# Start addresses of weight and activation tiles, and the place of each mixer unit's second transposition, in a two-block transformer kernel

## The chip, the cores and the metric

The kernel runs on one core of a Trainium2 chip, as one program. The metric is device time in microseconds (us): the median of a few executions. One further execution was taken with the hardware profiler, and all rows below come from it. Engines are named as the profile names them: PE is TensorE (PEld its weight loads), DVE is VectorE, ACT is ScalarE, POOL is GpSimd, SP is SyncE, whose queue starts most transfers.

## The reference, cut to what matters

256 tokens of width 2048 go through two transformer blocks, all in float32.

```
def first_block(x, mem, ...):
    xn = _rmsnorm(h, norm_mix)
    y = xn @ w_in                                  # 2048 x 7472
    mixed = concat(_gdn_group(y[..., :GDN_COLS]),  # gated delta rule, 8 heads of 128
                   _rwkv_group(y[..., GDN_COLS:])) # RWKV-7, 16 heads of 64
    h = h + mixed @ w_out
    h = h + _cross_attention(_rmsnorm(h), _rmsnorm(mem), wq, wk, wv, wo)
    h = h + square(relu(_rmsnorm(h) @ mlp_w_up)) @ mlp_w_down     # 2048 x 8192 x 2048
    return _rmsnorm(h, norm_final)

def second_block(x, ...):
    qa, ka, va, ga, qb, kb, vb, gb = split(x @ w_in)              # 2048 x 8192
    y = concat(dilated(qa, ka, va) * silu(ga), neighbourhood(qb, kb, vb) * silu(gb))
    return _layer_norm(ALPHA * x + y @ w_out)
```

## The kernel before, in words

Almost all of the work is the product of 256 tokens with about 390 MB of weights, which are read once. A weight piece of 256 rows by 512 columns comes in by one transfer (`raw`, three buffers). `piece` splits it in two float32r tiles: ACT writes the rounded half `whi`, DVE the rest `wlo = raw - whi`. Activations stand split in the same way (`ah`/`al`, `uh`/`ul`), and each product is three matmuls: high by high, high by low, low by high. A matmul has a stationary operand (128 columns that LDWEIGHTS puts into the array) and a moving one, which streams past it.

There are two forms. In `ws_parts` ("weights stationary") a 128x128 block of `whi` or `wlo` is stationary and 256 tokens of `ah` or `al` move: 256 columns a matmul, output by channel. In `as_parts` ("activations stationary") 128 tokens of `ah`, `al`, `uh` or `ul` are stationary and 512 columns of `whi` or `wlo` move. In the profile the moving operand is named first: `acc<-ah,whi` is the first form, `acc<-whi,ah` the second.

The pool `fix` lives through the whole program and holds `raw`, `whi`, `wlo`, one set of activation tiles and small constants. Other pools (`xn`, `work`, `act2`, `mlp`, `blk2`, `y`) are opened and closed by stage, and each begins where the pools that are open leave off.

From about 120 to 620 us the input projection runs interleaved with six mixer units: `rwkv_quarter(0)`, `(1)`, `gdn_half(0)`, `rwkv_quarter(2)`, `(3)`, `gdn_half(1)`. A unit is a chain of small steps on all engines. It is a generator whose yields (`yield cost, lat`) tell a planner in the same function how much PE work it has just issued and how much other PE work is to be put in before its next step; the planner fills with parts of the projection (0.66 each, six matmuls). PE's order is the one that this planner writes out. The other engines' orders are chosen by a scheduler when the program is built. Each unit ends with two halves of 128 tokens (c = 0 and 1). After the last product of a half (`op` in a quarter, `og` in a half) the output is normalized: DVE takes sums, POOL takes a power (`var` or `sso`, in `powc`), DVE multiplies, and then `finish(c)` transposes the result on PE (tiles `onp` or `ot`). `inverse_blocks` is a run of 62 operations on POOL (`Xt`, `X`), and the one of the following unit stands in the same POOL queue.

Of the kernel before, what the change touches and what calls it, by code (L numbers as in the profile page):

```python
# [9 lines left out]
F32 = mybir.dt.float32  # L10
F32R = mybir.dt.float32r
# [52 lines left out]
def block_kernel(tc, a, out, dbg=None, stop=99):  # L64
# [4 lines left out]
    def pool(name, space=None):  # L69
        kw = {"space": space} if space is not None else {"reuse_waits": "tile"}  # L70
        return ctx.enter_context(tc.tile_pool(name=name, bufs=1, **kw))

    def open_pool(name, side=None):
        cm = tc.tile_pool(name=name, bufs=1, side=side, reuse_waits="tile")
        return cm.__enter__(), lambda: cm.__exit__(None, None, None)

    fix = pool("fix")
    PS = {}

# [41 lines left out]

    last = {}

    def piece(W, r0, nk, cols):

        n = sum(c[1] for c in cols)
        with tc.high_priority():
            raw = fix.tile([128, nk, n], F32, name="raw", tag="raw", bufs=3)
            for c0, m, d in cols:
                nc.sync.dma_start(out=raw[:, :, d:d + m],  # L130
                                  in_=W[r0:r0 + nk * 128, c0:c0 + m].rearrange("(k p) n -> p k n", p=128))
            hi = fix.tile([128, nk, n], F32R, name="whi", tag="whi", bufs=3)
            lo = fix.tile([128, nk, n], F32R, name="wlo", tag="wlo", bufs=3)
            last["act"] = act(hi, raw)
            last["dve"] = nc.vector.tensor_tensor(out=lo, in0=raw, in1=hi.bitcast(F32), op=SUB)  # L135
        return hi, lo
# [8 lines left out]
    cst = fix.tile([128, K_END], F32, name="cst")  # L145
    nc.scalar.dma_start(out=cst[:, 0:128], in_=a["cst"][:, 0:128])
    pr0 = fix.tile([16, 128], F32, name="pr0")
    xnp, close_xn = open_pool("xn")
    xt = [xnp.tile([128, 2, 512], F32, name=f"xn{q}") for q in range(4)]
    lora_cols = [(7184, 288, 0), (4096, 16, 288)]  # L150
    first = []
    pr3 = fix.tile([75, 128], F32, name="pr3")
    nc.gpsimd.memset(pr3, 0.0)
    with tc.manual_schedule(engines={nc.sync.engine}):
        xq = pieces(a["x"], xt, (0,))
        nc.sync.dma_start(out=pr0, in_=a["norm_mix"][0].rearrange("(r c) -> r c", c=128))
        for qs in ((1,), (2,), (3,)):
            xq = pieces(a["x"], xt, qs)
            first.append(piece(a["w_in"][0], 256 * len(first), 2, lora_cols))
        nc.sync.dma_start(out=cst[:, 128:], in_=a["cst"][:, 128:])  # L160
        nc.sync.dma_start(out=pr3[0:26, :], in_=a["rwkv_mu"][0, 0:3328].rearrange("(r c) -> r c", c=128))
        nc.sync.dma_start(out=pr3[26:27, 0:32], in_=a["rwkv_mu"][0:1, 3328:3360])
        for i, n in enumerate(("rwkv_k_k", "rwkv_k_a", "rwkv_r_k", "rwkv_ln_w", "rwkv_ln_b", "rwkv_a0")):
            src = a[n][0].rearrange("h c -> (h c)") if n == "rwkv_r_k" else a[n][0]
            nc.sync.dma_start(out=pr3[27 + 8 * i:35 + 8 * i, :], in_=src.rearrange("(r c) -> r c", c=128))
# [48 lines left out]
    def act_tiles(where=None, bufs=8):  # L214

        hs, ls = [], []
        for _ in range(bufs // 2):
            h = (where or fix).tile([128, 4, T], F32R, name="ah", tag="act", bufs=bufs)
            l = (where or fix).tile([128, 4, T], F32R, name="al", tag="act", bufs=bufs)
            hs += [h[:, i, :] for i in range(4)]  # L220
            ls += [l[:, i, :] for i in range(4)]
        return hs, ls
# [17 lines left out]
                tr(p[:, t * 128:(t + 1) * 128], src(t, k // 4)[:, (k % 4) * 128:(k % 4) * 128 + 128])  # L240
            split(p, hs[k], ls[k], gain[:, k:k + 1])

    def by_channel(p, name):

        n = p.shape[0]
        q = pst([128, 128], "parp")
        tr(q[:, 0:n], p)
        o = fix.tile([128, n], F32, name=name)
        nc.vector.tensor_copy(o, q[:, 0:n])
        return o  # L250

    gains = {"mix": by_channel(pr0, "par0")}

    def ws_parts(W, cols, xh, xl, emit, kts=None, r0=0, needs=(), first=()):


        total = sum(c[1] for c in cols)
        n = -(-total // 128)
        acc = [mmt([128, 2, T], "acc") for _ in range((n + 1) // 2)]
        kts = kts or list(range(len(xh)))  # L260
        nk = 2
        for i in range(0, len(kts), nk):
            hi, lo = first[i // nk] if i // nk < len(first) else piece(W, r0 + kts[i] * 128, nk, cols)
            for c in range(n):
                cc = slice(c * 128, min(c * 128 + 128, total))
                o = acc[c // 2][0:cc.stop - cc.start, c % 2, :]
                for j in range(nk):
                    k = kts[i + j]
                    mm(o, hi[:, j, cc], xh[k], start=(i + j == 0 and c % 2 == 0), stop=False)
                    mm(o, hi[:, j, cc], xl[k], start=False, stop=False)  # L270
                    mm(o, lo[:, j, cc], xh[k], start=False, stop=(i + j == len(kts) - 1 and (c % 2 == 1 or c == n - 1)))
                yield PART
        yield from needs
        with tc.high_priority():
            for c in range(n):
                emit(c, acc[c // 2][:, c % 2, :])
# [39 lines left out]
    w_in = a["w_in"][0]  # L316
# [3 lines left out]
    r0 = rstd(xq, "r0")  # L320
# [34 lines left out]
    normw = bcast("normw", a["gdn_norm_w"][0], 128)  # L355


    work_p, close_work = open_pool("work")

    def wk(shape, name, bufs=1, dt=F32):  # L360
# [193 lines left out]
    def rwkv_quarter(qt):  # L554
# [149 lines left out]
        for c in range(2):  # L704
            rp_ = pst([128, 4, 64], "rp_")
            for h in range(4):
                if c == 1 and h % 2 == 0:
                    mm(rp_[:, h:h + 2, :], AR[:, h // 2, 1, 0, :], zs[:, h // 2, :], stop=False)
                mm(rp_[:, h, :], L[h][:, 1, :], vtok[:, c, h, :], start=(c == 0), stop=(c == 0 or h % 2 == 1))
            rs = wk([128, 4, 64], "rs")  # L710
            act(rs, rp_)
            yield 0.45 + 0.4 * c, 1.3
            up = pst([128, 4, 64], "up")
            for h in range(4):
                mm(up[:, h, :], tinv[:, c * 4 + h, :], rs[:, h, :])
            us = wk([128, 4, 64], "us")
            nc.vector.tensor_copy(us, up)
            yield 0.45, 1.5
            op = pst([128, 4, 64], "op")
            for h in range(4):  # L720
                if c == 1 and h % 2 == 0:
                    mm(op[:, h:h + 2, :], AR[:, h // 2, 1, 1, :], zs[:, h // 2, :], stop=False)
                mm(op[:, h, :], L[h][:, 0, :], us[:, h, :], start=(c == 0), stop=False)
                mm(op[:, h, :], L[h][:, 2, :], vtok[:, c, h, :], start=False, stop=(c == 0 or h % 2 == 1))
            if c == 0:
                zp = pst([128, 2, 64], "zp")
                for h in range(4):
                    i, e = h // 2, slice(64 * (h % 2), 64 * (h % 2) + 64)
                    mm(zp[e, i, :], btok[:, h, :], us[:, h, :], stop=False)
                    mm(zp[e, i, :], ktok[:, h, :], vtok[:, 0, h, :], start=False)  # L730
                for h1 in range(2):
                    e = slice(64 * h1, 64 * h1 + 64)
                    tt(zs[e, :, e], zp[e], zsc[e].unsqueeze(2).to_broadcast([64, 2, 64]), MUL)

            mean = wk([128, 4], "mean", bufs=2)
            nc.vector.tensor_reduce(out=mean, in_=op, axis=AX.X, op=ADD)
            ts(mean, mean, 1.0 / 64, MUL)
            o_ = wk([128, 4, 64], "oc")
            oc.append(o_)
            tt(o_, op, mean.unsqueeze(2).to_broadcast([128, 4, 64]), SUB)  # L740
            osq = wk([128, 4, 64], "rs")
            act(osq, o_, AF.Square)
            var = wk([128, 4], "var", bufs=2)
            nc.vector.tensor_reduce(out=var, in_=osq, axis=AX.X, op=ADD)
            ts(var, var, 1.0 / 64, MUL, 64e-5, ADD)
            powc(var, var, mhalf[:, 0:4])
            tt(o_, o_, var.unsqueeze(2).to_broadcast([128, 4, 64]), MUL)
            if c == 0:
                yield 1.5, 0.5
                for i in range(2):  # L750
                    lmats(1, i)
                    yield 1.3, 2.5 * i
                finish(0)
                yield 0.22, 0
            else:
                yield 0.9, 7.0
                finish(1)
                yield 0.22, 0
        done.add(("end", f"q{qt}"))
# [33 lines left out]
    def gdn_half(hf):  # L793
# [156 lines left out]
        tt(o_[1], p, o_[1], ADD)  # L950
        norm(1)
        done.add(("gq", hf))
        yield 2.2, 9.0
        finish(1)
        done.add(("gz", hf))
        yield 0.45, 0
# [461 lines left out]
            attention(grp, hf)  # L1418
    close_at()
    yp, close_y = open_pool("y")  # L1420
    for more, x in zip(act_tiles(yp, 4), (yh, yl)):
        x += more
    for grp in range(2):
# [75 lines left out]
```

## Time and profile before

| | |
|---|---|
| time, median of 3 runs | 2284.04 us (2282.37 to 2285.6) |
| the profiled execution's own time | 2280.03 us |
| its span, first to last instruction | 2278.3 us |
| PE busy | 2215.0 us, 97% of the span |
| DVE, ACT, POOL busy | 1385.3, 1119.9, 272.5 us |
| mean granted PE clock | 0.990 of full speed |

Busy time counts an instruction from its start to its (modelled) end; matmuls overlap each other, so their durations add up to more than PE's busy time. What a matmul takes of the span is the distance from its start to the next one's.

### The profile page before, as it was taken

To read this page: it belongs to the slowest core of one execution; us is meant where nothing else is said; L and a number is where in the kernel's file an instruction comes from. 1 tells how busy PE (TensorE), PEld (TensorE's weight loads), DVE (VectorE), ACT (ScalarE), POOL (GpSimd) and SP (SyncE) were. 2 spreads that over 40 slices of the span, in tenths; PEclk is the share of its full clock that TensorE was granted. 3 is DMA by queue.
4 is the path that set the end of the run, shared out by engine and by line. 5 is a ranking of instruction groups with operands and counts; after the bars stand their busy time and mean duration, and the time that the engine had idled before them with its cause. 6 is when DMAs were issued, how large, how long until landed. Compare 5 with 4: busy or idle time off the path is not lost.

```text
span 2278.3 us, 39054 instructions
## 1 busy us (share of the span) xinstructions
PE 2215.0 (97%) x15506; PEld 2013.3 (88%) x15506; DVE 1385.3 (61%) x2236; ACT 1119.9 (49%) x1802; POOL 272.5 (12%) x540
## 2 busy tenths in 40 slices
PE   8999999899999999999999999999999999999996
PEld 8998888889988899889998898898888999889975
DVE  5576676675644556555554455455456677777765
ACT  5455454554444545454444444344344565656542
POOL 0027255345200000000000000000000000022101
PEclk9999999999999999999999999999999999999998
DMA  6554244344466554456665665565556666665553
GB/s 209 185 162 123 94 153 130 105 147 129 143 211 205 183 171 148 155 181 183 189 188 185 186 188 189 186 186 188 189 183 197 197 189 188 183 181 167 178 191 130
DMA packets 229060, 391.77 MB, mean 172 GB/s; under 512 B 39886, under 2 KB 47820, under 8 KB 228493
## 3 DMA queue, kind: packets, MB, share of 16 engines
q1 hardware_dynamic: 227297, 385.63, 55.0%
q10 hardware_dynamic: 1036, 3.58, 0.4%
q8 instruction: 121, 1.98, 0.4%
q14 instruction: 62, 0.51, 0.1%
q0 software_dynamic: 544, 0.07, 0.0%
HBM read 386.25 MB, written 2.97 MB: 171 GB/s over the span
## 4 chain that ended last, share of the span: by engine, by line
PE 85%; POOL 5%; DVE 3%; DMA 2%; ACT 2%; issue 2%; SPq 0%; POOLq 0%; ACTq 0%; DVEq 0%
PE acc L96 78%; POOL X L102 2%; POOL Xt L102 2%; DVE wlo L135 1%; DMA raw<-in_w_in_dram 1%; DMA nb<-scr 1%; PE s2p L96 1%; PE o2p L96 1%; PE t2p L178 1%; PE xo L96 1%; PE xs L96 0%; PE tp L178 0%; ACT whi L99 0%; DMA kT<-in_mem_dram 0%; DVE h L111 0%
## 5 line engine op out<-in xcount | busy, mean ns | idle before, releaser
L135 DVE TENSOR_TENSOR wlo<-raw,whi 128x1024 fp32r<-128x1024 f32 (+1 forms) x696 | 852.2, 1225 | 718.0 <-ACT whi L99 711.8
L99 ACT ACTIVATE whi<-raw 128x1024 fp32r<-128x1024 f32 (+1 forms) x696 | 734.2, 1056 | 884.4 <-PE acc L96 771.6
L96 PE MATMUL acc<-ah,whi 128*128 128x256 f32 x3120 | 883.7, 284 | 2.2 <-DVE ey L102 1.2
L96 PE MATMUL acc<-ah,wlo 128*128 128x256 f32 x3120 | 872.0, 280 | 3.4 <-DVE wlo L135 3.3
L96 PE MATMUL acc<-al,whi 128*128 128x256 f32 x3120 | 874.8, 281 | 0.0
L96 PEld LDWEIGHTS acc<-ah,whi 128*128 128x128 f32 x3120 | 588.0, 188 | 7.6 <-issue 2.3
L96 PEld LDWEIGHTS acc<-ah,wlo 128*128 128x128 f32 x3120 | 586.3, 188 | 4.9 <-DVE wlo L135 4.8
L96 PEld LDWEIGHTS acc<-al,whi 128*128 128x128 f32 x3120 | 587.8, 188 | 1.4 <-issue 0.9
L96 PE MATMUL acc<-wlo,ah 128*128 128x512 f32 x704 | 278.7, 396 | 0.0
L96 PE MATMUL acc<-whi,al 128*128 128x512 f32 x704 | 278.4, 396 | 0.0
L96 PE MATMUL acc<-whi,ah 128*128 128x512 f32 x704 | 268.7, 402 | 4.0 <-DVE qky L102 2.6
L96 PE MATMUL acc<-wlo,uh 128*128 128x512 f32 x512 | 202.4, 395 | 0.0
L96 PE MATMUL acc<-whi,ul 128*128 128x512 f32 x512 | 202.3, 395 | 0.0
L96 PE MATMUL acc<-whi,uh 128*128 128x512 f32 x512 | 182.5, 395 | 0.0
L96 PEld LDWEIGHTS acc<-whi,ah 128*128 128x128 f32 x704 | 132.3, 189 | 34.5 <-DVE qky L102 2.8
L96 PEld LDWEIGHTS acc<-whi,al 128*128 128x128 f32 x704 | 132.6, 188 | 31.7
L96 PEld LDWEIGHTS acc<-wlo,ah 128*128 128x128 f32 x704 | 133.0, 189 | 30.3
L96 PEld LDWEIGHTS acc<-wlo,uh 128*128 128x128 f32 x512 | 96.0, 188 | 23.4
L96 PEld LDWEIGHTS acc<-whi,ul 128*128 128x128 f32 x512 | 96.1, 188 | 23.2
L96 PEld LDWEIGHTS acc<-whi,uh 128*128 128x128 f32 x512 | 95.9, 187 | 23.3
L102 POOL TENSOR_TENSOR Xt<-X,nb 128x60 f32<-128x60 f32 (+24 forms) x186 | 76.4, 411 | 181.8 <-DMA nb<-scr 163.5
L1342 POOL MEMSET klz<- 64x256 f32 x8 | 2.5, 307 | 714.9 <-DMA raw<-in_w_in_dram 714.6
(523 smaller groups left out, 1858.5 us busy)
## 6 DMA issues: line engine op xcount, KB each, us to landing
raw<-in_w_in_dram SPq DMA_DIRECT2D x240, 512.0 KB, 3.8
raw<-in_mlp_w_up_dram SPq DMA_DIRECT2D x128, 512.0 KB, 3.7
raw<-in_mlp_w_down_dram SPq DMA_DIRECT2D x128, 512.0 KB, 3.8
raw<-in_w_out_dram SPq DMA_DIRECT2D x64, 512.0 KB, 4.4
raw<-in_xattn_wk_dram SPq DMA_DIRECT2D x32, 512.0 KB, 3.8
raw<-in_xattn_wv_dram SPq DMA_DIRECT2D x32, 512.0 KB, 4.9
raw<-in_xattn_wq_dram SPq DMA_DIRECT2D x32, 512.0 KB, 4.1
raw<-in_xattn_wo_dram SPq DMA_DIRECT2D x32, 512.0 KB, 3.7
```

The lines of the kernel that those rows point to most:

```text
L96: nc.tensor.matmul(o, l, r, start=start, stop=stop)
L99: return nc.scalar.activation(o, i, f, **kw)
L102: (eng or nc.vector).tensor_tensor(out=o, in0=x, in1=y, op=op)
L135: last["dve"] = nc.vector.tensor_tensor(out=lo, in0=raw, in1=hi.bitcast(F32), op=SUB)
L178: nc.tensor.transpose(o, i, ident[0:n, 0:n])
L1342: nc.gpsimd.memset(kl[other, e, :].bitcast(F32), 0.0)
```

## The change

Three things are changed. (1) `whi` and `wlo` are allocated 256 B longer per partition, and `piece` has an offset `o` in elements: where weights are stationary (`ws_parts`, and the first pieces) the view begins 56 elements, that is 224 B, into the tile; in `as_parts` it begins at 0. (2) Fillers (`shift`) of 160, 96 and 128 B, and a small tile that is allocated earlier, put `fix`'s big tiles and the pools behind it at multiples of 256 B. (3) Two yields before `finish(1)` ask for more work ahead: 7.0 becomes 9.0 in a quarter, 9.0 becomes 13.0 in a half.

```diff
+    def shift(where, nbytes):
+        if nbytes:
+            where.tile([128, nbytes // 4], F32, name=f"shift{nbytes}")
...
-    def piece(W, r0, nk, cols):
+    def piece(W, r0, nk, cols, o=0):
...
-            hi = fix.tile([128, nk, n], F32R, name="whi", tag="whi", bufs=3)
-            lo = fix.tile([128, nk, n], F32R, name="wlo", tag="wlo", bufs=3)
+            hi, lo = (fix.tile([128, nk * n + 64], F32R, name=x, tag=x, bufs=3)[:, o:o + nk * n]
+                      .rearrange("p (k n) -> p k n", k=nk) for x in ("whi", "wlo"))
...
     pr0 = fix.tile([16, 128], F32, name="pr0")
+    par0 = fix.tile([128, 16], F32, name="par0")
+    shift(fix, 160)
...
-            first.append(piece(a["w_in"][0], 256 * len(first), 2, lora_cols))
+            first.append(piece(a["w_in"][0], 256 * len(first), 2, lora_cols, 56))
...
-            hi, lo = first[i // nk] if i // nk < len(first) else piece(W, r0 + kts[i] * 128, nk, cols)
+            hi, lo = first[i // nk] if i // nk < len(first) else piece(W, r0 + kts[i] * 128, nk, cols, 56)
...
+    shift(fix, 96)
     work_p, close_work = open_pool("work")
...
             else:
-                yield 0.9, 7.0
+                yield 0.9, 9.0
                 finish(1)
...
-        yield 2.2, 9.0
+        yield 2.2, 13.0
         finish(1)
...
     yp, close_y = open_pool("y")
+    shift(yp, 128)
```

Where the two built programs put the operands, as the remainder of the start address by 256 B (all steps inside a tile are multiples of 512 B, so the remainder is the same for every matmul of a line; "distance" is stationary less moving, by 256):

| matmuls | moving, stationary, distance before | after |
|---|---|---|
| weights stationary, 256 columns (all stages) | 96, 32, 192 | 0, 224, 224 |
| activations stationary, tiles in `act2`, `mlp` (`w_out`, `wo`, `w_down`) | 32, 0, 224 | 0, 0, 0 |
| activations stationary, tiles in `fix` (z, `wv`, v of block 2) | 32, 96, 64 | 0, 0, 0 |
| activations stationary, tiles in `blk2`, `y` (last projection) | 32, 0 or 128, 224 or 96 | 0, 0, 0 |
| cross-attention scores `xs` | 96, 64, 224 | 0, 64, 64 |
| block 2 scores `s2p` | 128, 128, 0 | 128, 128, 0 |

On PE the instructions are the same, and the mixer units' are moved. At the end of the first quarter (`op` is its last product, `onp` the second transposition, `gamp` belongs to the following unit), before, with 66 matmuls of the projection left out or shown between `op` and `onp`:

```order
L96 MATMUL op<-us,og 128x64
L96 MATMUL op<-p2d,og 128x64
L96 MATMUL acc<-ah,whi 128x256
...
L96 MATMUL acc<-ah,wlo 128x256
L178 MATMUL onp<-cst,oc 128x128 x2
L96 MATMUL gamp<-cst,g 128x128 x4
```

and after, with 84 between them:

```order
L101 MATMUL op<-us,og 128x64
L101 MATMUL op<-p2d,og 128x64
L101 MATMUL acc<-ah,whi 128x256
...
L101 MATMUL acc<-ah,wlo 128x256
L186 MATMUL onp<-cst,oc 128x128 x2
L101 MATMUL gamp<-cst,g 128x128 x4
```

So 18 projection matmuls have moved ahead of the transposition, and with it of all that stands behind. It is 18 in the second and third quarter too, 6 in the fourth (66 become 72), and 36 in both halves (84 become 120, between `og` and `ot`).

On POOL the scheduler has put one power in another place. In the third quarter, the power of the second half (`var`) stands before behind seven pairs of the following unit's inverse (`Xt`, `X`):

```order
L680 AFFINE_SELECT og<-og 128x2x128
L102 TENSOR_TENSOR Xt<-X,nb 128x31
L102 TENSOR_TENSOR X<-X,Xt 128x31
...
L102 TENSOR_TENSOR Xt<-X,nb 128x2x25
L102 TENSOR_TENSOR X<-X,Xt 128x2x25
L182 TENSOR_TENSOR var<-var,cst 128x4
L102 TENSOR_TENSOR Xt<-X,nb 128x2x24
```

and after it stands ahead of all of them:

```order
L687 AFFINE_SELECT p2c<-p2c 128x128
L689 AFFINE_SELECT p2c<-p2c 128x2x128
L687 AFFINE_SELECT og<-og 128x128
L689 AFFINE_SELECT og<-og 128x2x128
L190 TENSOR_TENSOR var<-var,cst 128x4
L107 TENSOR_TENSOR Xt<-X,nb 128x31
L107 TENSOR_TENSOR X<-X,Xt 128x31
```

In the fourth quarter the same power moves the other way: before, the last two pairs of the inverse stand behind it,

```order
L102 TENSOR_TENSOR X<-X,Xt 128x8x3
L182 TENSOR_TENSOR var<-var,cst 128x4
L102 TENSOR_TENSOR Xt<-X,nb 128x8x2
L102 TENSOR_TENSOR X<-X,Xt 128x8x2
L102 TENSOR_TENSOR Xt<-X,nb 128x8
L102 TENSOR_TENSOR X<-X,Xt 128x8
```

and after, they stand ahead of it:

```order
L107 TENSOR_TENSOR X<-X,Xt 128x8x3
L107 TENSOR_TENSOR Xt<-X,nb 128x8x2
L107 TENSOR_TENSOR X<-X,Xt 128x8x2
L107 TENSOR_TENSOR Xt<-X,nb 128x8
L107 TENSOR_TENSOR X<-X,Xt 128x8
L190 TENSOR_TENSOR var<-var,cst 128x4
```

## Rows read from the trace of the kernel before

**Rows 1.** The page: PE's busy time, and the chain's shares by engine

```profile
PE 2215.0 (97%) x15506; PEld 2013.3 (88%) x15506; DVE 1385.3 (61%) x2236; ACT 1119.9 (49%) x1802; POOL 272.5 (12%) x540
...
PE 85%; POOL 5%; DVE 3%; DMA 2%; ACT 2%; issue 2%; SPq 0%; POOLq 0%; ACTq 0%; DVEq 0%
```

**Rows 2.** Groups by shape, whole span: count | busy us, mean ns | idle before

```profile
L96 PE MATMUL acc<-ah,whi 128*128 128x256 f32 x3104 | 879.3, 284 | 2.2 <-DVE ey L102 1.2 <-ACT whi L99 0.9
L96 PE MATMUL acc<-al,whi 128*128 128x256 f32 x3104 | 870.5, 281 | 0.0
L96 PE MATMUL acc<-ah,wlo 128*128 128x256 f32 x3104 | 868.3, 280 | 3.4 <-DVE wlo L135 3.3
...
L96 PE MATMUL acc<-whi,al 128*128 128x512 f32 x704 | 278.4, 396 | 0.0
...
L96 PE MATMUL acc<-whi,ul 128*128 128x512 f32 x512 | 202.3, 395 | 0.0
...
L96 PE MATMUL s2p<-k,q 128*128 128x256 f32 x64 | 16.9, 284 | 0.0
...
L96 PE MATMUL xs<-kv,qx 128*128 128x256 f32 x96 | 14.2, 280 | 0.0
```

**Rows 3.** The chain in order of time, three stretches: start us, us, what

```profile
587.34 5.65 PE acc L96 x48
...
595.22 9.53 PE acc L96 x84
...
841.67 2.24 PE xs L96 x19
...
979.71 22.40 PE acc L96 x96
```

**Rows 4.** Groups by shape in 650 to 740 us, and at two form changes

```profile
L96 PE MATMUL acc<-whi,al 128*128 128x512 f32 x128 | 50.6, 395 | 0.0
...
L96 PE MATMUL acc<-whi,al 128*128 128x512 f32 x1 | 0.4, 389 | 0.0
...
L96 PE MATMUL acc<-whi,al 128*128 128x512 f32 x1 | 0.4, 398 | 0.0
```

**Rows 5.** PE's timeline at four second transpositions: start us, us [idle before <-releaser]

```profile
245.45 0.33 PE L178 MATMUL onp<-cst,oc 128*128 128x128 f32 x1 [2.85 <-DVE oc L102]
...
389.08 0.59 PE L178 MATMUL ot<-cst,og 128*128 128x128 f32 x2 [3.43 <-DVE og L111]
...
448.30 0.66 PE L178 MATMUL onp<-cst,oc 128*128 128x128 f32 x2 [4.86 <-DVE oc L102]
...
545.36 0.41 PE L178 MATMUL onp<-cst,oc 128*128 128x128 f32 x2 [2.01 <-DVE oc L102]
```

**Rows 6.** Timeline of POOL and DVE ahead of the last two

```profile
439.32 0.60 POOL L102 TENSOR_TENSOR Xt<-X,nb 128x31 f32<-128x31 f32 x1 [10.93 <-DMA nb<-scr]
...
442.43 0.20 DVE L108 TENSOR_SCALAR var<-var 128x4 f32<-128x4 f32 x1
...
446.61 1.02 POOL L182 TENSOR_TENSOR var<-var,cst 128x4 f32<-128x4 f32 x1
...
447.66 0.49 DVE L102 TENSOR_TENSOR oc<-oc,var 128x256 f32<-128x256 f32 x1 [2.58 <-POOL var L182]
...
543.73 1.02 POOL L182 TENSOR_TENSOR var<-var,cst 128x4 f32<-128x4 f32 x1
...
546.53 0.22 POOL L102 TENSOR_TENSOR X<-X,Xt 128x8 f32<-128x8 f32 x1
```

**Rows 7.** Stretches: us, busy by engine (count), granted PE clock, DMA share, GB/s

```profile
391.00:394.00 3.00, 3.00 (x16) 3.00 (x15) 3.00 (x8) 1.04 (x3) 0.00 (x0) 0.50 0.37 109
448.40:452.30 3.90, 3.90 (x19) 3.90 (x20) 1.03 (x3) 2.15 (x4) 3.19 (x10) 0.50 0.00 0
```

**Rows 8.** The fourth quarter's `xd`: durations min/median/max ns, first to last start

```profile
L96 PE MATMUL py<-xd,nt x32: 191/191/212, 499.1 to 499.6; 32*32 32x32 f32 x32
...
L99 ACT ACTIVATE xd<-Xt x4: 307/320/323, 483.9 to 486.0; 32x64 f32<-32x64 f32 x4
```

More of the change, by code (lines that the diff above doesn't have):

```diff
@@ L241, in transposed, with by_channel @@
             split(p, hs[k], ls[k], gain[:, k:k + 1])
-    def by_channel(p, name):
+    def by_channel(p, name, o=None):
         n = p.shape[0]
@@ L247, in by_channel @@
         tr(q[:, 0:n], p)
-        o = fix.tile([128, n], F32, name=name)
+        o = o if o is not None else fix.tile([128, n], F32, name=name)
         nc.vector.tensor_copy(o, q[:, 0:n])
         return o
-    gains = {"mix": by_channel(pr0, "par0")}
+    gains = {"mix": by_channel(pr0, "par0", par0)}
     def ws_parts(W, cols, xh, xl, emit, kts=None, r0=0, needs=(), first=()):
```

## The prediction

> **What bounds the kernel now.** I read the page first [rows 1]: PE is busy for 2215.0 of 2278.3 us and makes 85% of the chain that ends last. So only two things can move the time: how far apart matmuls start while PE streams, and how long PE stands still, or runs at half clock, because of a wait. I then read the groups by shape [rows 2]. Nearly all of PE's time is two shapes: 3 x 3104 = 9312 matmuls of 256 columns (weights stationary), and 3 x 704 + 3 x 512 = 3648 of 512 columns (activations stationary). Their idle time is a few us in all, so transfers and the splitting on ACT and DVE are hidden.
>
> Durations overlap, so for spacing I went to the chain [rows 3], whose pieces are unbroken. 48 matmuls of 256 columns took 5.65 us, 117.7 ns each; a few us later 84 of the same took 9.53 us, 113.5 ns each. The 512-column ones took 22.40/96 = 233.3 ns. The reader is to see that one shape, at the same remainders by 256 B and the same clock, has two steady rhythms, 4.2 ns apart, and keeps one until something else comes between. Durations follow spacings (280 ns goes with 117.7, 395 with 233.3), so I use them where a spacing can't be read.
>
> Last, PE's waits [rows 5]. Four second transpositions stood still for 2.85, 3.43, 4.86 and 2.01 us, 13.15 us together; the second quarter's and the second half's did not wait. [...]
>
> **The change part by part.** *Later transpositions.* 18 matmuls more are 18 x 117.7 ns = 2.1 us, 36 are 4.2 us, 6 are 0.7 us. That work is taken from behind the wait, so what it covers is a gain, up to the wait itself.
> - First quarter: 2.1 of 2.85 us are covered: -2.1.
> - First half: 4.2 us cover all of 3.43, and the low clock behind it should not come: -3.4 - 1.1 = -4.5.
> - Third quarter: 2.1 of 4.86 would be covered, but POOL's order changes too. DVE had the input of the power ready at 442.63, and POOL did it at 446.61, since it went on with the inverse from 439.32 [rows 6]. Now the power comes first: done at about 442.63 + 1.02 = 443.65. DVE's queue was empty from 447.66 - 2.58 = 445.08 on, so the product (0.49 us) ends at about 445.6; PE stood from 448.30 - 4.86 = 443.44 on, and now arrives 2.1 later, at 445.6. So I take the wait and its low clock as gone: -4.9 - 1.7 = -6.6.
> - What is late next: the inverse starts some 4.3 us later, behind the power. It feeds `xd`, complete at 486.0 + 0.3, which PE took at 499.1 [rows 8]: 12.8 us of cover, less 4.3 and the 6.6 that PE gains. It holds. Without this cover each us would be PE's.
> - Fourth quarter: two more pairs of the inverse stand ahead of the power. Before, they ran behind it, until 546.53 + 0.22 = 546.75; the power ended at 544.75, so it is 2.0 us later, and PE arrives 0.7 later: +1.3.
> - Second quarter and second half: no wait before, none now: 0.
>
> Sum: -2.1 - 4.5 - 6.6 + 1.3 = -11.9 us. Bounds: -13.15 - 2.8 = -16 if all of it goes, +3 if the waits only change place and the fourth one brings a low clock (1.7) besides its 1.3.
>
> *Weights stationary, 9312 matmuls.* Both operands move; the distance goes from 192 to 224. The nearest row is `xs`: 256 columns, float32r, distance 224. It streams at 2.24/19 = 117.9 ns [rows 3], with a mean of 280 ns [rows 2], as the projections do. I take 0. From below: the faster rhythm, -4.2 x 9312 = -39 us (a little less, since some stretches have it). From above: `s2p`, whose moving operand starts at a multiple of 64 B, as all will now, has 284 ns against 280: +4 x 9312 = +37 us.
>
> *Activations stationary, 3648 matmuls.* The distance becomes 0. Before, distances of 64 and 224 gave the same 395 ns [rows 2, 4], so most distances seem to be alike. Distance 0 occurs in the program where this form is followed by the other: the last 512-column matmul then runs while `whi` is loaded from the same remainder as the moving `whi`. There are seven such places, with durations of 389 (three), 392, 393, 394 and 398 ns, the first and the last of that order in [rows 4]; the mean is 392.0, 3 ns under 395. Single steps are weak evidence for a rhythm, but they are nearest in shape. I take -3 x 3648 = -11 us; bounds: -6 and +3 ns, -22 and +11 us.
>
> [...]
>
> *All else:* longer tiles and fillers cost no instruction; ACT's and DVE's writes keep their sizes, with the 39% of the span in which DVE idles [rows 1] as cover; if the split lagged behind PE, PE's wait for `wlo`, 3.4 us before [rows 2], would grow by the lag.
>
> Sum: -11.9 + 0 - 11 = -23 us on the profiled execution's 2280.0 us (span 2278.3). That execution is 4.0 us under the median of the runs shown, 2284.0; against the median the forecast is **2261 us**. Its own range is 2246 (all waits gone, -22) to 2276 (-11.9 shrinks to -8, no effect of addresses).
>
> **The rivals.** *(A) The new addresses put the 256-column stream into its faster rhythm.* For it: that rhythm exists, 113.5 ns, so nothing forbids it. Against it: `xs` at the new distance has the slower one. Time: 2261 - 39 = 2222; with the 512-column term at its bound and all waits gone, 2284 - 16 - 39 - 22 = 2207.
>
> *(B) Addresses do nothing:* the rhythm is set by when the two reads start, and the change leaves that alone. For it: at 512 columns distances 64 and 224 are alike before [rows 2, 4], at 256 columns 192 and 224 [rows 2]. Against it: the seven steps at distance 0. Time: 2284 - 11.9 = 2272. [...]
>
> *(C) The other side: multiples of 64 B are the bad place.* `s2p`, at distance 0 and such a start, is 4 ns slower than the projections [rows 2]. If every 256- and 512-column matmul paid that, it is 4 x 12960 = +52, and 2284 - 12 + 52 = 2324. It decides from 0.9 ns a matmul on (11.9 / 12960). Against it: `s2p` comes in short groups between waits, so its mean holds more than the rhythm.
>
> *(D) The transpositions' waits only move on and addresses do nothing:* 2284.
>
> **How the numbers follow.** Chances: forecast 0.38, A 0.28, B 0.18, C 0.11, D 0.05. The range of 2207 to 2284 runs from A's low end to D; it leaves out C and the tails of A, under 2 in 10. Below 0.2% (4.6 us; the three runs lie 3.2 us apart) a measurement can't tell a change. Faster: forecast, A and nearly all of B, 0.80; same: D and rests of B and C, 0.08; slower: C, 0.12.
>
> **What would show it.** Right: the chain's pieces of 512-column matmuls at about 230 ns (392 ns duration), those of 256 columns still at 117.7 (280); the four waits down from 13.15 us to about 4, with `onp` in the third quarter free of waits and no stretch of clock 0.50 near 391 and 448 us. A: durations of 276 in all projections. B: 395 and 280 everywhere. C: 284 and 399. The prediction is wrong if the spacing changes in the 256-column form, 9312 of 15506 matmuls, in either direction; or if the later inverse makes PE wait at `py`.

## The result and the profile after

The changed kernel takes 2256.41 us (median of four runs, 2250.71 to 2262.2), the kernel before beside it 2283.20 us: 26.8 us less, ratio 0.9877 with a 95% interval of 0.9859 to 0.9896. The forecast was 2261 us. The total came out close, but none of its three terms did, as the experiments show: the 512-column form gave nearly twice its forecast, the transpositions about a fifth, and some 5 us came where nothing was forecast. The profiled execution is the longest of the four runs, 2262.2 us; 17.8 us under the profiled execution of before. Its stretches at granted clock 0.50 add up to about 64 us, those of before to about 44 (read in windows of 2 us; the first expectation below has 69 and 40).

The page of the changed kernel, PE's busy time and the chain's shares (answers to [rows 1]):

```profile
PE 2200.2 (97%) x15506; PEld 2019.2 (89%) x15506; DVE 1389.2 (61%) x2236; ACT 1120.5 (50%) x1802; POOL 269.4 (12%) x540
...
PE 87%; DVE 4%; DMA 3%; POOL 3%; ACT 2%; issue 1%; SPq 0%; POOLq 0%; ACTq 0%; DVEq 0%
```

Groups by shape, whole span (answers to [rows 2]):

```profile
L101 PE MATMUL acc<-ah,whi 128*128 128x256 f32 x3104 | 881.1, 284 | 2.5 <-DVE ey L107 1.8 <-ACT whi L104 0.7
...
L101 PE MATMUL acc<-whi,al 128*128 128x512 f32 x704 | 275.8, 392 | 0.0
...
L101 PE MATMUL acc<-whi,ul 128*128 128x512 f32 x512 | 199.2, 389 | 0.0
```

By durations the 512-column form gained 4 to 6 ns and the 256-column form nothing. The chain's unbroken pieces (start us, us, what; answer to [rows 3]) say more. Of the changed kernel:

```profile
55.87 54.24 PE acc L101 x464
...
747.43 21.78 PE acc L101 x96
...
1020.44 644.34 PE acc L101 x4321
```

and of the kernel before, the two pieces with which the first and the third compare (the second compares with the last line of [rows 3]):

```profile
54.71 54.75 PE acc L96 x464
...
1024.30 656.13 PE acc L96 x4321
```

96 matmuls of 512 columns take 21.78 us, 226.9 ns each, where [rows 3] has 22.40 and 233.3. So the spacing fell by 6.5 ns, a little more than the durations show. The 464 of 256 columns went from 118.0 to 116.9 ns. The third piece is the MLP up to its last block, both forms mixed: 11.8 us less, with the same work.

The four waits of [rows 5] are gone, and the granted clock behind the transpositions is 1.00. PE's timeline at the four, then windows behind the second and the third (the places of [rows 7]):

```profile
244.90 0.38 PE L186 MATMUL onp<-cst,oc 128*128 128x128 f32 x2
...
390.91 0.60 PE L186 MATMUL ot<-cst,og 128*128 128x128 f32 x4
...
456.54 0.38 PE L186 MATMUL onp<-cst,oc 128*128 128x128 f32 x2
...
552.81 0.38 PE L186 MATMUL onp<-cst,oc 128*128 128x128 f32 x2
```

```profile
391.00:396.00 5.00, 5.00 (x45) 5.00 (x44) 4.74 (x15) 3.52 (x7) 0.00 (x0) 1.00 0.34 103
456.50:461.50 5.00, 5.00 (x45) 5.00 (x45) 2.52 (x5) 2.82 (x4) 4.29 (x10) 1.00 0.56 152
```

But PE waits at places where it hardly did before. The same timeline, seven such places:

```profile
281.51 0.43 PE L101 MATMUL rp__3614<-p2d,og 128*128 128x64 f32 x2 [1.26 <-POOL og L687]
...
345.46 0.21 PE L101 MATMUL pz<-xt,y 32*32 32x32 f32 x1 [1.09 <-DVE y L520]
...
372.36 1.47 PE L186 MATMUL ot<-cst,og 128*128 128x128 f32 x4 [1.96 <-DVE og L116]
...
435.46 0.41 PE L186 MATMUL onp<-cst,oc 128*128 128x128 f32 x2 [2.14 <-DVE oc L107]
...
439.84 1.10 PE L101 MATMUL up<-rs,tinv 128*128 128x64 f32 x8 [1.59 <-ACT rs L104]
...
500.46 0.66 PE L186 MATMUL bkp<-cst,wB 128*128 128x128 f32 x4 [1.83 <-DVE al L116]
...
531.37 0.44 PE L186 MATMUL onp<-cst,oc 128*128 128x128 f32 x2 [2.42 <-DVE oc L107]
```

Together 12.3 us, where before the same places had 1.6, against the 13.15 that went. So from the trace alone theory 1 was: the addresses made the gain, most of it in the 512-column form, and the transpositions' waits moved on. Theory 2 was the prediction's own sum (transpositions 11.9, 512-column form 11). The kernel before ran on the same chip beside each kernel below; ratios are against it, with a 95% interval behind them.

### The profile page after: what moved, and what is told of

Same layout as the page of the kernel before. It is cut to its first block, busy times and chain, and to the rows that moved or that the text cites. A ratio compares the mean times of both kernels' runs of the same rounds, so it can differ in the third digit from the quotient of the medians.

```text
span 2260.5 us, 39043 instructions
## 1 busy us (share of the span) xinstructions
PE 2200.2 (97%) x15506; PEld 2019.2 (89%) x15506; DVE 1389.2 (61%) x2236; ACT 1120.5 (50%) x1802; POOL 269.4 (12%) x540
## 4 chain that ended last, share of the span: by engine, by line
PE 87%; DVE 4%; DMA 3%; POOL 3%; ACT 2%; issue 1%; SPq 0%; POOLq 0%; ACTq 0%; DVEq 0%
PE acc L101 79%; POOL Xt L107 1%; DMA raw<-in_w_in_dram 1%; POOL X L107 1%; DVE wlo L141 1%; PE o2p L101 1%; PE s2p L101 1%; DMA nb<-scr 1%; PE t2p L186 1%; PE op L101 1%; PE xs L101 0%; PE xo L101 0%; ACT whi L104 0%; PE tp L186 0%; DMA rT<-in_mem_dram 0%
```

## The experiments

### Which part of the change

*Addresses only* (the changed kernel with its two yields back):

```diff
-                yield 0.9, 9.0
+                yield 0.9, 7.0
-        yield 2.2, 13.0
+        yield 2.2, 9.0
```

> The changed kernel with its two yields put back to 7.0 and 9.0, so that only the addresses differ from the kernel before. Theory 1, from the trace after: the 512-column matmuls gave all of their bound (3648 x 6.3 ns = 23 us), the 256-column ones some 0.4 ns each (4 us), and the later transpositions gave nothing, since their waits came back elsewhere and the low clock grew from 40 to 69 us of the span. Then this kernel is at 2283 - 27 = 2256 us, or down to 2250 if the transpositions cost up to 6 us; low-clock stretches as before. Theory 2, the prediction: the later transpositions give 12 us and the addresses 11; then it is at 2283 - 11 = 2272 us.

Measured: 2255.93 us, the kernel before 2281.53: ratio 0.9891 (0.9878 to 0.9905), 25.6 us less. Theory 1.

*Transpositions only* (the kernel before with 9.0 and 13.0):

> The kernel before with the two yields at 9.0 and 13.0 and nothing else. Theory 1: 2283 to 2289 us (no gain, or a loss by waits that move on and by low clock). Theory 2: 2283 - 12 = 2271 us.

Measured: 2279.13 us, ratio 0.9989 (0.9979 to 1.0000), 2.4 us less: far from 12, and a little better than theory 1, though the interval runs from 0 to 4.8 us.

*Weights stationary at distance 192, as before* (addresses only; `56` becomes `48` in `ws_parts` and for the first pieces):

> The addresses only (yields as before), but the weights' views begin at 192 B where weights are stationary, so that the distance there is 192 as it was before; where activations are stationary it stays 0. Theory 1: 512-column durations 392 ns, and 2260 us (only the 23 us), or 2256 if the 4 us of the 256-column form do not hang on the distance. Theory 2: 2272 us.

Measured: 2254.58 us, ratio 0.9885 (0.9872 to 0.9899), 1.4 us under the addresses of the change, which is no difference. Yet the spacing did change; the chain's MLP piece:

```profile
1014.69 647.67 PE acc L101 x4321
```

That is 3.3 us more than at 224 (644.34 above, and 644.35 with the addresses only). Block 2 gives it back: between its first chain piece of 286 matmuls and its last of 34 it takes 392.5 us (1740.55 to 2133.05), with the addresses only 396.95 (1737.61 to 2134.56). Its pieces of 56 matmuls take 6.35 us there, against 6.54 to 6.60: the faster rhythm that the last section shows.

*Activations stationary at distance 224, as in most stages before* (addresses only):

```diff
-                w.append(piece(W, r0 + kts[i * nk] * 128, nk, [(c0, 512, 0)]))
+                w.append(piece(W, r0 + kts[i * nk] * 128, nk, [(c0, 512, 0)], 8))
```

> The addresses only (yields as before), but the weights' views begin at 32 B where activations are stationary, so that the distance there is 224 as in most stages before; where weights are stationary it is 224 as in the changed kernel. Theory 1: 512-column durations back at 395 to 396 ns, and 2283 - 4 = 2279 us. Theory 2: 2283 us. If the gain came from the pools' multiples of 256 B and not from the distance, it would stay near 2256 with 392 ns.

Measured: 2276.06 us, ratio 0.9976 (0.9967 to 0.9985). So the 512-column form alone is worth 20.1 us, and 5.5 us (3.4 to 7.5) hang on the rest of the layout. Chain of this kernel (the 96 are of 512 columns, the last piece is the MLP's):

```profile
52.86 54.25 PE acc L101 x464
...
744.89 22.40 PE acc L101 x96
...
1021.68 652.77 PE acc L101 x4321
```

The 512-column piece is back at before's 22.40, the 256-column one has kept its gain. The MLP piece is 3.4 us under before's 656.13, with 512 columns at distance 224 in both: this is what the 256-column form gave there, and it is most of the 5.5.

### Distance or start, and which distance

*All starts 32 B on, distances kept* (addresses only):

```diff
-    shift(fix, 160)
+    shift(fix, 192)
```

> The addresses only (yields as before), with one filler 32 B longer: all big tiles and all later pools begin 32 B further on, so every distance stays as in the changed kernel (0 and 224) and only the starts move from 0 to 32. Theory 1a, the distance between the two operands sets the spacing: 512-column durations stay at 389 to 392 ns, and 2256 us. Theory 1b, a start at a multiple of 64 B (or 256 B) of the moving weights sets it: durations back at 395 to 397 ns and 2256 + 20 = 2276 us. In the 256-column form, 280 to 281 ns either way; if the 0.4 ns of spacing hang on the start, up to 4 us more.

Measured: 2255.80 us, the kernel before 2280.38: ratio 0.9892 (0.9871 to 0.9912). In its chain 96 of 512 columns take 21.78 us and the 464 take 54.24, as in the changed kernel. So for this step of 32 B it is the distance between the two operands that sets the spacing, and not where they start; other steps were not tried.

*Two maps of distances* (addresses only, with an offset for each stage). In the first:

```diff
+    off = {"ws": 56, "as": 0}
...
+        off["ws"] = (0, 16, 32, 8)[b]
...
+        off["as"] = (16, 32, 48, 56)[b]
```

> The addresses only (yields as before), with another offset of the weights' views in some stages, so that one run shows many distances. Weights stationary: w_up in four blocks at distances 0, 64, 128, 32; wq at 96; block 2 at 160. Activations stationary: w_down in four blocks at distances 192, 128, 64, 32; last projection at 96; the rest at 0. Theory 1, only distance 0 is good where 512 columns stream: 395 to 396 ns in all four blocks of w_down, against 389 to 390 in the changed kernel. If nearness counts, 32 lies between. For 256 columns, theory 1 (the distance does nothing) has 280 to 281 ns in all four blocks of w_up; the rival, that distance 0 is good there too, has about 276 to 277 in the first block alone.

The second is the same with `(52, 60, 50, 54)[b]` and `(1, 2, 4, 60)[b]`:

> As the map of distances, with other offsets. Weights stationary: w_up in four blocks at distances 208, 240, 200, 216; wq at 176; block 2 at 248. Activations stationary: the moving weights of w_down begin 4, 8, 16 and 240 B into their tile (distances 252, 248, 240 and 16), those of the last projection 24 B. If what matters where 512 columns stream is that both operands stand at the very same place modulo 256 B, already 4 B gives 395 ns; if it is the same 64 B, the first three stay at 389 to 392 and the fourth is at 395. For 256 columns: the map had the shortest spacing at 224 and the longest at 0 and 160; if 224 is the bottom of one dip, 208, 216 and 240 have 280 to 281 ns and 248 tends to 284; if it is a point of its own, they are longer.

Windows of 70 us each inside one block of one form; the number to read is PE's count. First map (`w_up` 0 and 1, `w_down` 0, `w_up` 2, `w_down` 1):

```profile
1020.00:1090.00 70.00, 70.00 (x586) 70.00 (x585) 37.11 (x47) 33.19 (x48) 0.00 (x0) 1.00 0.62 182
1110.00:1180.00 70.00, 70.00 (x597) 70.00 (x596) 39.29 (x51) 33.65 (x52) 0.00 (x0) 1.00 0.63 188
1200.00:1270.00 70.00, 70.00 (x301) 56.70 (x300) 31.61 (x28) 30.63 (x35) 0.00 (x0) 1.00 0.58 188
1290.00:1360.00 70.00, 70.00 (x593) 70.00 (x592) 37.67 (x47) 32.78 (x48) 0.00 (x0) 1.00 0.63 187
1380.00:1450.00 70.00, 70.00 (x303) 56.72 (x303) 35.96 (x37) 27.40 (x28) 0.00 (x0) 1.00 0.59 188
```

Second map (`w_up` 0 and 1, `w_down` 0):

```profile
1020.00:1090.00 70.00, 70.00 (x603) 70.00 (x602) 38.33 (x48) 33.45 (x49) 0.00 (x0) 1.00 0.63 187
1110.00:1180.00 70.00, 70.00 (x586) 70.00 (x585) 38.12 (x49) 33.48 (x51) 0.00 (x0) 1.00 0.61 184
1200.00:1270.00 70.00, 70.00 (x295) 55.65 (x294) 31.96 (x30) 29.81 (x34) 0.00 (x0) 1.00 0.58 183
```

With the addresses of the change the same windows hold 602 or 603 matmuls of 256 columns (distance 224) and 310 or 311 of 512 (distance 0), so it is not the stage that makes the difference. Addresses only, the second and the third window:

```profile
1110.00:1180.00 70.00, 70.00 (x602) 70.00 (x601) 39.01 (x50) 34.06 (x51) 0.00 (x0) 1.00 0.63 188
1200.00:1270.00 70.00, 70.00 (x310) 57.99 (x309) 32.21 (x27) 30.43 (x34) 0.00 (x0) 1.00 0.61 195
```

256 columns, both maps: 603 at 208, 597 at 64 and 200, 594 at 32, 593 at 128, 586 at 0 and 240, 585 at 216; the run at 192 has 596 or 597. So the theory that this distance does nothing is wrong, and so is its rival: 0 is among the worst, and good and bad places lie 8 B apart (208, 216, 224). 512 columns: 301 to 303 at distances 192, 128 and 64; with the moving operand only 4, 8 and 16 B into its tile 295, 302 and 304. Of the places tried only the very same remainder is good. The two maps took 2279.17 and 2278.35 us in one execution each and serve for spacings alone.

*Distance 0 in both forms* (addresses only, no offset where weights are stationary):

> The addresses only, but with no offset where weights are stationary: distance 0 in both forms. By the map (256 columns: 120.0 ns at distance 0 against 117.0 at 224, from start to start) this is 9312 x 3.0 = 28 us slower than the addresses of the change, 2256 + 28 = 2284 us, about the kernel before. By the theory that the distance does nothing where weights are stationary: 2256 us.

Measured: 2278.07 us, the kernel before 2282.02: ratio 0.9984 (0.9975 to 0.9993). That is 22 us more than the addresses of the change; the forecast from the map was 28. The chain's 464 matmuls:

```profile
53.88 55.77 PE acc L101 x464
```

120.2 ns each, against 116.9 at 224. The offset of 224 B where weights are stationary makes no gain over 192 that the whole time shows, but without it the multiples of 256 B would have cost nearly all that they bring.

### The transpositions one by one

All four have the addresses of the change. *Third quarter alone*, and *first half alone*:

```diff
-                yield 0.9, 7.0
+                yield 0.9, 13.0 if qt == 2 else 7.0
```

```diff
-        yield 2.2, 9.0
+        yield 2.2, 13.0 if hf == 0 else 9.0
```

> The addresses only, with one yield changed: in the third quarter 13.0 in place of 7.0, so that 54 more projection matmuls (6.4 us) stand ahead of its second transposition, all taken from a stretch of 132 ahead of the next unit's first product, which leaves 78. Nothing else moves on PE in the mixers, and POOL's order is as before. If a wait that is covered by work from a stretch which itself covers nothing is a gain, 4.86 us of wait and 1.7 us of low clock go: 2256 - 6.6 = 2249 us. If waits only move on, 2256.

> The addresses only, with 13.0 in place of 9.0 in the first half alone. 36 more matmuls stand ahead of its second transposition; PE's order then takes 36 from the stretch of 132 behind the third quarter, but also 42 from the 168 ahead of the fourth quarter's py, and the planner weaves the fourth quarter and the second half in another way. Theory 2, the prediction: 3.4 us of wait and 1.1 of low clock go, 2256 - 4.5 = 2251 us. Theory 1, the waits move on: new waits of 1 to 2 us each at bkp and onp of the fourth quarter as in the run with both yields, and 2254 to 2258 us.

Measured, in the same set of runs in which all starts 32 B on gave 2255.80 us: third quarter 2251.05 us (ratio 0.9865, 0.985 to 0.988), first half 2255.36 us (0.9883, 0.9865 to 0.9901). The third quarter's wait is gone and 4.8 us with it; the slowest of its four executions (2251.21) is quicker than the quickest with these addresses alone (2252.83 here, 2254.76 in the earlier set). The first half's move takes its wait and its low clock away in the changed kernel (1.00 from 391 to 396 us); alone it shows no gain, though the interval of some 4 us to either side nearly reaches the 4.5 that was forecast.

Where that went is seen in the changed kernel's trace, which has the same move. Its windows, then those of addresses only, over the third quarter's small products:

```profile
396.00:400.60 4.60, 3.92 (x56) 3.09 (x54) 4.60 (x9) 3.43 (x8) 0.00 (x0) 1.00 0.67 191
400.60:414.20 13.60, 13.60 (x101) 9.88 (x98) 8.16 (x23) 4.45 (x14) 2.13 (x7) 0.50 0.17 54
```

```profile
396.00:410.00 14.00, 14.00 (x176) 11.67 (x169) 10.38 (x24) 7.50 (x19) 3.26 (x8) 1.00 0.18 62
```

and the first and the last of one run of instructions, the same in both, in the changed kernel and in addresses only:

```profile
402.44 0.51 PE L101 MATMUL pz<-xt,y 32*32 32x32 f32 x3
...
414.30 1.14 PE L101 MATMUL pz<-tinv,ty 64*64 64x64 f32 x16
```

```profile
398.02 0.22 PE L101 MATMUL pz<-xt,y 32*32 32x32 f32 x2
...
404.53 1.14 PE L101 MATMUL pz<-tinv,ty 64*64 64x64 f32 x16
```

11.86 us against 6.51: the stretch fell to half clock, after 4.6 us in which PE was idle for 0.7, and lost 5.4 us. With the first half alone the low clock holds even over 400 to 420 us:

```profile
400.00:420.00 20.00, 20.00 (x138) 15.76 (x137) 10.66 (x25) 5.50 (x15) 2.84 (x8) 0.50 0.12 42
```

The three profiled executions with this move (the changed kernel, the first half alone, the transpositions only) have a mean granted clock of 0.986, all others 0.988 to 0.991. That every execution with the move has the low stretch is not shown: the profiled one of the first half alone is the slowest of its four, and two of the others, at a mean clock of 0.989, took 2252.79 and 2253.68 us, like the two of all starts 32 B on at 0.990 (2252.83 and 2254.09). So the new waits may eat the gain by themselves. With the first half alone there are waits of 1.83 us at `bkp` and of 2.38 at the fourth quarter's first `onp`, which addresses only does not have.

The first half's move also does most of what the prediction put down to the third quarter's. With the first half alone the third quarter's second `onp` waits 1.05 us, where addresses only has 4.86:

```profile
456.72 0.41 PE L186 MATMUL onp<-cst,oc 128*128 128x128 f32 x2 [1.05 <-DVE oc L107]
```

In the changed kernel POOL stands idle ahead of that power, and the inverse behind it waits for its own input:

```profile
449.17 1.01 POOL L190 TENSOR_TENSOR var<-var,cst 128x4 f32<-128x4 f32 x1 [12.01 <-DVE var L113]
...
451.90 0.24 POOL L107 TENSOR_TENSOR Xt<-X,nb 128x31 f32<-128x31 f32 x1 [1.73 <-DMA nb<-scr]
```

*First and third quarter*: the yield is `(9.0, 7.0, 13.0, 7.0)[qt]`.

> The third quarter's yield at 13.0, and the first quarter's at 9.0 as in the changed kernel; the rest as before. 18 more matmuls stand ahead of the first quarter's second transposition, six each taken from stretches of 24, 48 and 54 behind it. Theory 2 (a covered wait is a gain): 2.1 of the 2.9 us, 2251 - 2.1 = 2249 us. Theory 1 (what is taken from stretches that cover later waits comes back there): 2251 us, with longer waits at the products behind it.

Measured: 2248.07 us, ratio 0.9850 (0.9837 to 0.9863): 34.0 us under the kernel before, the best version here, 8.3 us under the changed kernel by the medians. The first quarter's wait of 2.9 us became one of 1.26 at `rp` and one of 1.33 at `pz`. The step from 2251.05, in another set of runs, is 3.0 us by the medians and 4.6 against the kernel before of each set, and both intervals reach some 3 us to either side, so its size is not shown.

*All four quarters at 9.0, halves as before*:

> The addresses of the change and its yield of 9.0 in all four quarters; the halves stay at 9.0 as before. On PE the quarters' second transpositions move as in the change (18 matmuls each), and the weaving of the fourth quarter with the second half, which the first half's yield changes, is nearly as before. If the change's gain by the quarters is lost through the first half's yield: first quarter 3.0 us (as measured alone), third quarter 2.1 to 3.8 us (18 matmuls of its 4.86 us, and at most its low clock), fourth quarter 0 to 2.0: 2256 - 5 to 8 = 2248 to 2251 us, without the waits at bkp and the fourth quarter's first onp. If waits simply move on whichever yield is raised: 2255 to 2256 us.

Measured: 2254.24 us, the kernel before 2283.98: ratio 0.9880 (0.9863 to 0.9896). Between the two expectations, and no clear gain over addresses only. The third quarter shows why; POOL and then PE in it:

```profile
439.74 0.40 POOL L107 TENSOR_TENSOR Xt<-X,nb 128x31 f32<-128x31 f32 x1 [13.92 <-DMA nb<-scr]
...
446.79 1.02 POOL L190 TENSOR_TENSOR var<-var,cst 128x4 f32<-128x4 f32 x1
```

```profile
448.49 0.66 PE L186 MATMUL onp<-cst,oc 128*128 128x128 f32 x2 [4.84 <-DVE oc L107]
```

The power still stands behind the inverse in POOL's queue, and the inverse starts when its input lands, 3.2 us later than in addresses only (436.51). 18 matmuls more ahead, and the wait is as long as ever: without the first half's move they do not remove it.

PE's waits of 0.3 us or more from 100 to 640 us, added up from each run's timeline, say the same: addresses only 21.5 us, first half alone 20.7, all four quarters 21.2, third quarter alone 17.7, first and third 16.0; the kernel before has 22.4 and the changed kernel 18.6, with more low clock. Where the time fell clearly, waits went; with the first half alone and with all four quarters they stand in other places.

## Why the prediction was right in sum, and where it was wrong

**Activations stationary: right in mechanism, half the size.** The term was -11 us from "-3 ns each". The matmuls lost 22.40/96 - 21.78/96 = 6.5 ns, 3648 x 6.5 = 24 us; undone, it costs 20.1. The mis-sized step is the mean over seven form-change matmuls: their durations ran from 389 to 398, and the three of 389 were the steady value at distance 0, which the changed kernel has in the MLP (`acc<-whi,ul` above). Why 24 by the spacing is 20.1 by the time was not looked into.

**Weights stationary: size nearly right, reason wrong.** The term was 0; what the addresses gain beside the 512-column form is 5.5 us, of which 3.4 are seen in this form's spacing in the MLP. "I take 0" rested on `xs` at distance 224 streaming as the projections at 192 do, and on the view that most distances are alike. They are not: at distance 208 there are 603 matmuls in 70 us, at 0 there are 586, and distance 0 throughout costs 22 us. 192 and 224 happen to lie near each other, with 597 and 603. By the prediction's own test (the 256-column spacing changes) this step failed, and with it, in its own words, the prediction. Rival A's stream at 113.5 ns did not come. Rival C's price is near what distance 0 costs (120.2 against 116.9 ns), but its reason is not: starts at multiples of 64 B, moved by 32 B, made no difference. Nor did its row show a price of the address: `s2p` has a median duration of 280 ns, and its mean of 284 comes from a few of up to 420. Rival B, by which addresses do nothing, does not hold: a change of distance alone moved the whole kernel by 20 us in the one form and by 22 in the other. What makes the distance matter, no run shows.

**Later transpositions: -11.9 forecast, -2.4 measured.** The step that failed is "That work is taken from behind the wait, so what it covers is a gain, up to the wait itself". The waits went as forecast, and the low clock right behind them. But the matmuls came out of stretches that covered other waits, and the planner wove the fourth quarter in another way: all of PE's waits together fell from 22.4 to 18.6 us, not by the 13.15 of the four. Term by term: the first quarter's -2.1 is not contradicted (3.0 by the medians, within the noise); the third's -6.6 has 4.8 with 54 matmuls taken from a stretch of 132 that had room, but with its 18 and the other quarters' its wait stays, and it went only where the first half's move was there too; the first half's -4.5 does not show, since new waits and, in the traced executions, low clock on small products further on (5.4 us) stand against it. That place was not looked at, since the prediction followed the clock only where the wait stood. The fourth quarter's +1.3 and the second half's 0 were not tried alone. No run shows the 1.1 and 1.7 us for low clock that the sum contains. What the runs showed in their place: 45 matmuls in 5.00 us at clock 1.00 behind the first half's and the third quarter's transposition, and 4.8 us in all for the third quarter's wait together with its low clock.

**The cover of the later inverse: right that it holds, wrong in size.** In the changed kernel `xd` is complete at 489.8 + 0.2 = 490.0 us, and PE takes it at 502.7 ([rows 8] has 486.3 and 499.1). So 12.7 us of the 12.8 are left, where the prediction's figures leave 1.9. PE does wait at `py`, 0.73 us, but for DVE's `wB`.

So -20, -5.5 and -2.4, 28 us together where the whole change shows 26.8, stand for the -11, 0 and -11.9 that were forecast. The errors have opposite signs, and that the total came within 5 us is luck.

## What to carry to other kernels

Where matmuls stream back to back, look up the remainders by 256 B of both operands and try a few distances: here a step of 4 or 8 B is worth 3 to 5% of the streaming time (603 matmuls against 585, 310 against 295), it differs by form, and 0 was best for 512 columns and among the worst for 256. Try them on one run with another offset in each stage, and read counts in equal windows; durations show it poorly. Before filler is moved ahead of a wait, ask what that filler covers now, and take it from where there is room; then look at the granted clock over the next stretch of small products, not only behind the wait.

## What was not expected of the hardware

The 256-column form keeps one of two rhythms at distance 192. In the run with that distance, most long pieces of block 2 stand in the fast one, the first piece in the slow one, and the scores `xs`, which that run left alone, are fast:

```profile
52.59 54.75 PE acc L101 x464
...
834.94 2.15 PE xs L101 x19
...
2062.94 7.71 PE acc L101 x68
```

118.0 and 113.4 ns for the first and the last, at the same addresses. The kernel before has distance 192 too, with other starts, and streams the like of the last piece in the slow rhythm; the changed kernel has the same `xs` at the same addresses, and slow:

```profile
2086.33 8.01 PE acc L96 x68
```

```profile
839.91 2.24 PE xs L101 x19
```

That is 113.2 and 117.9 ns for `xs`, where the two runs differ in the weights' offset and the yields alone. So what runs around it has a part in its rhythm, and the row on which the forecast's "I take 0" stood was no clean measure of its own distance. At 224 most long pieces of block 2 lie between 116.5 and 118.1 ns. What chooses the rhythm, and why a distance of a few bytes between two operands matters, stays open. In the chains of the kernel before, the changed kernel and the runs on addresses no long piece came below 113.2 ns.
